# Weight sums of the FFN's down projection in half blocks on another engine, and the layer norm's channel sums as split matmuls

## The chip, the cores and the metric

The kernel runs on one core of a Trainium2 chip. The metric is the device time of one execution in microseconds (us). The core has five engines that run side by side, each with its own queue of instructions, worked off in order: TensorE (PE, matmuls), VectorE (DVE), ScalarE (ACT), GpSimd (POOL) and SyncE (SP, which here only starts DMA transfers). SBUF is the on-chip memory that the engines work from, PSUM the memory into which TensorE writes its products, and DRAM the large memory outside.

## What is computed

One residual block on x of 512 frames by 1024 channels, all in float32:

```
h   = rmsnorm(x); proj = h @ w_in                      # 1024 -> 8208 columns
a   = gated delta rule over 8 heads of 128, chunks of 64, then rmsnorm and silu(z)
c   = ga * sigmoid(gb); c = causal depthwise conv of 31 taps (c) + bias
c   = silu(layernorm over the 1024 channels (c))       # mean and variance of each frame
x   = x + (gate_a * (a @ w_o) + gate_b * (c @ w_pw2 + b)) @ w_out
h2  = rmsnorm(x)
f   = silu(h2 @ w_gate) * (h2 @ w_up)                  # 1024 -> 2 x 2816
out = rmsnorm(x + f @ w_down)                          # 2816 -> 1024
```

## The kernel before

**Products.** Activations lie with channels on the 128 partitions and the 512 frames along the free axis (128x512 tiles). A product in float32 accuracy is made of three faster ones: each operand is split into a rounded half (type fp32r) and the rest, `hi` and `lo`, and `split3` (L117) multiplies hi·hi, hi·lo and lo·hi. For weights this is done by `unit` (L101): SP loads 128x1024 into `raw`, ACT copies it rounded into `whi` (L113), DVE subtracts to get `wlo` (L114). The pool `wp` has three buffers of each, so the load of a unit waits until DVE is through with the `raw` of three units before, and the copy into `whi` waits until TensorE is through with the old one.

**Layer norm.** The convolution of 31 taps runs on DVE in the background of the first stage and ends in eight tiles `cv`; DVE adds them up into `sacc` (L704). Behind the first of eight column blocks of `a @ w_o`, `ln_mean` (L715) multiplies `sacc` by a matrix of ones, so that every partition holds the sum over the channels; it subtracts the mean and adds up the squares in `vacc`. Behind the fourth block `ln_norm` (L731) does the same with `vacc`, and scales. These two matmuls (L717, L733) take plain float32 operands and run as two instructions each. The tile name `acc4` is that of the short convolution's accumulators, two buffers in the pool `tp`.

**FFN.** Both FFN products use a recursive scheme that saves one of eight block products, for which sums and differences of weight blocks are needed. For gate and up, DMAs that add as they write make these sums in DRAM (`s1` to `s4`). For down, `w_down` comes in 11 row blocks k of four 128x512 sub-blocks each; `dsums_load` (L168) loads them, `dsums_add` (L171) makes four sums in place, and a DMA from POOL's queue stores them to `wsum[k]` in DRAM. That is done in 22 half blocks `halves` (k and one half of 512 columns) where there is room: 14 of them before the FFN, in buffers called `U` and `wsh`. The eight left (`rest`, k = 7 to 10) are done while gate and up run.

That stage is a loop over pairs f = 3 to 21 (L1180): `pair(f)` takes four units (loads from `wgu` and `s1` to `s4`; the last of the four has 128x512) and seven products of 12 matmuls with 256 columns; `dsums_to(f)` (L1069) does a part of `rest`; `some_operands(f)` makes the rounded halves `fh` and `fl` of finished hidden tiles `fm`, from f = 11 on with a difference `s` on DVE and two operations on POOL ahead. Before, `dsums_to` takes whole blocks of 128x4x512 in f = 8, 11, 14 and 17, in one buffer `wst`: the load on SP behind the last unit of the pair, the four sums and the store on POOL.

**Order.** The program is written once for all engines; each engine gets its instructions in about the order of the source, moved by priorities, and waits on semaphores for its inputs and for the buffers that it writes. `tc.issue_after(x)` keeps an instruction behind x on the same engine, and `behind()` behind the last marked ones of each engine.

Of the kernel before, what the change touches and what calls it, by code (L numbers as in the profile page):

```python
# [6 lines left out]
F32 = mybir.dt.float32  # L7
F32R = mybir.dt.float32r
I32 = mybir.dt.int32
AF = mybir.ActivationFunctionType  # L10
ALU = mybir.AluOpType
# [3 lines left out]
P = 128  # L15
T = 512
# [16 lines left out]
def block_kernel(ctx, tc, a):  # L33
    nc = tc.nc
    V, S, G, PE = nc.vector, nc.scalar, nc.gpsimd, nc.tensor
# [16 lines left out]
    ident, tri, suf, mid, ones, neg = (cst[:, i * P:(i + 1) * P] for i in range(6))  # L52
# [17 lines left out]
    one = small.tile([P, 1], F32, name="one")  # L70
# [14 lines left out]
    def marked(b, kind="drain"):  # L85
        mark[b.ins.engine, kind] = b.ins
        return b

    @contextmanager
    def behind(only=None):  # L90
        with ExitStack() as st:
            for i in list(mark.values()):
                if only is None or i.engine == only:
                    st.enter_context(tc.issue_after(i))
            yield
# [35 lines left out]
    psm = ctx.enter_context(tc.tile_pool(name="psm", bufs=3, space=PSUM))  # L131
# [4 lines left out]
    tp = keep.enter_context(tc.tile_pool(name="tp", bufs=2))  # L136
# [7 lines left out]
    cs = []  # L144
# [23 lines left out]
    def dsums_load(k, r, eng, cs=slice(0, T)):  # L168
        eng.dma_start(r, a["wdn"][k].rearrange("p (i c) -> p i c", i=4)[:, :, cs])

    def dsums_add(k, r, cs=slice(0, T)):  # L171
        b11, b12, b21, b22 = (r[:, i, :] for i in range(4))
        with tc.issue_after(last[0].ins):
            for o, x, y in ((b22, b12, b22), (b12, b11, b12), (b11, b22, b11), (b21, b11, b21)):
                G.tensor_tensor(out=o, in0=x, in1=y, op=ALU.add)  # L175
        nc.gpsimd.dma_start(wsum[k][:, :, cs], r)

    def half_load():
# [24 lines left out]
    def fill():  # L203

        units[0] += 1
        if units[0] % 3 != 2 or not gps_:
            feed_one()
        if taken and units[0] % 3 != 2 and not norming[0]:
            dsums_add(*taken.pop(0))
        if halves and gps_ and units[0] > 3 and not taken and not norming[0] and (units[0] % 2 == 0 if len(gps_) == 1 else units[0] % 3 == 0):  # L210
            half_load()
# [3 lines left out]
    with tc.tile_pool(name="st", bufs=2) as st:  # L215
# [78 lines left out]
        ps = psg.tile([P, 4, P], F32, name="g")  # L294
# [8 lines left out]
        raw, hi, lo = early[3]  # L303
# [41 lines left out]
        for k in range(2, 4):  # L345
# [6 lines left out]
                        in1=ss[:, 1].rearrange("p (n a) -> p n a", a=1).broadcast_to([P, NT, 16]), op=ALU.mult)  # L352
# [6 lines left out]
                        in1=rowp[:, 1:2, :].broadcast_to([P, NT, H]), op=ALU.add)  # L359
# [9 lines left out]
        with tc.issue_after(ln_.ins):  # L369
            for g_ in gated:  # L370
# [8 lines left out]
                        op=ALU.mult)  # L379
# [313 lines left out]
    sacc = tp.tile([P, T], F32, name="sacc", bufs=1)  # L693
# [14 lines left out]
    def gate(i):  # L708
# [3 lines left out]
        nc.sync.dma_start(sgd[i], sg)  # L712
        yield

    def ln_mean():  # L715
        ps = psm.tile([P, T], F32, name="mm")
        PE.matmul(ps, ones, sacc, start=True, stop=True)  # L717
        mu = tp.tile([P, T], F32, name="pa", bufs=1)
        S.activation(mu, ps, AF.Copy, scale=1.0 / D)
        vacc = tp.tile([P, T], F32, name="sacc", bufs=1)  # L720
        for i in range(KD):
            V.tensor_tensor(out=cv[i], in0=cv[i], in1=mu, op=ALU.subtract)
            if i == 0:
                S.activation(vacc, cv[i], AF.Square)
            else:
                sq2 = tp.tile([P, T], F32, name="acc4")
                S.activation(sq2, cv[i], AF.Square)
                V.tensor_tensor(out=vacc, in0=vacc, in1=sq2, op=ALU.add)
        return vacc

    def ln_norm(vacc):  # L731
        ps = psm.tile([P, T], F32, name="mm")
        PE.matmul(ps, ones, vacc, start=True, stop=True)  # L733
        rstd = tp.tile([P, T], F32, name="pa", bufs=1)
        S.activation(rstd, ps, AF.Sqrt, scale=1.0 / D, bias=epsc)
        V.reciprocal(out=rstd, in_=rstd)
        for i in range(KD):
            V.tensor_tensor(out=cv[i], in0=cv[i], in1=rstd, op=ALU.mult)
            S.activation(cv[i], cv[i], AF.Silu, scale=ln_w[:, i:i + 1], bias=ln_b[:, i:i + 1])
# [102 lines left out]
    def others():  # L842
        for i in range(2, KD):
            yield from glu(i)
        yield from gates(0, 16)
# [9 lines left out]
    rest = others()  # L855
# [30 lines left out]
    mp = ph2.enter_context(tc.tile_pool(name="mp", bufs=2))  # L886
    mp.tile([P, PAD], F32, name="pad", bufs=1)
    while taken:
        dsums_add(*taken.pop(0))
# [8 lines left out]
    def split(src):  # L898
        hi = mp.tile([P, T], F32R, name="yh", bufs=KD)
        lo = mp.tile([P, T], F32R, name="yl", bufs=KD)  # L900
        S.activation(hi, src, AF.Copy)
        V.tensor_tensor(out=lo, in0=src, in1=hi.bitcast(F32), op=ALU.subtract)
        return hi, lo

    mas = []
    oh, ol = zip(*[split(zall[:, k, :]) for k in range(KD)])
    for j in range(KD):
        if j == 1:
            vacc = ln_mean()
        if j == 4:  # L910
            ln_norm(vacc)
            norming[0] = False
        ps = psm.tile([P, T], F32, name="mm")
        col_tile(ps, a["wo"][j], oh, ol)
        ma = mp.tile([P, T], F32, name="ma", bufs=KD + 1)
        V.tensor_tensor(out=ma, in0=ps, in1=gate_of(j), op=ALU.mult)
        mas.append(ma)
# [7 lines left out]
    for j in range(KD):  # L925
        ps = psm.tile([P, T], F32, name="mm")
# [92 lines left out]
    while taken:  # L1019
        dsums_add(*taken.pop(0))  # L1020
    gps_.clear()
    rest = [(k, cs) for k, cs in halves]
# [5 lines left out]
    TH, KH = T // 2, KD // 2  # L1028
    t1, t2 = slice(0, TH), slice(TH, T)
    fp = ctx.enter_context(tc.tile_pool(name="fp", bufs=FF))  # L1030
    fs = ctx.enter_context(tc.tile_pool(name="fs", bufs=1))
# [10 lines left out]
    def tt(out, in0, in1, op, eng=V):  # L1042
        return eng.tensor_tensor(out=out, in0=in0, in1=in1, op=op)  # L1043
# [9 lines left out]
    def operands(f):  # L1053
# [12 lines left out]
        tt(b[:, t2], b[:, t1], b[:, t2], ALU.subtract, G)  # L1066
        tt(b[:, t1], b[:, t2], fm[:, t2], ALU.add, G)

    def dsums_to(f):  # L1069
        if f > 7 and f % 3 == 2 and rest:  # L1070
            k, cs = rest.pop(0)
            if rest and rest[0][0] == k:
                rest.pop(0)
                cs = slice(0, T)
            r = fs.tile([P, 4, T], F32, name="wst")[:, :, 0:cs.stop - cs.start]
            with tc.issue_after(loads[-1].ins):
                dsums_load(k, r, nc.sync, cs)
            dsums_add(k, r, cs)

# [36 lines left out]
    for f in range(F0):  # L1118
        start_feed[0] = f > 0
        dsums_to(f)  # L1120
        if f > 1:
            pg = psm.tile([P, T], F32, name="mm")
            col_tile(pg, a["wgu"][f], hhk, hlk)
        else:
            pg = first[2 * f][0]
            k_loop(*first[2 * f], slice(2 * P, T))
        sg = fq.tile([P, T], F32, name="cw", bufs=2)
        S.activation(sg, pg, AF.Silu)
        if f:
            next_todo()  # L1130
            pu = psm.tile([P, T], F32, name="mm")
            col_tile(pu, a["wgu"][FF + f], hhk, hlk)
        else:
            pu = first[1][0]
            k_loop(*first[1], slice(2 * P, T))
        tt(hidden(), pu, sg, ALU.mult)
        next_todo()
# [42 lines left out]
    for f in range(F0, FF):  # L1180
        pair(f)
        dsums_to(f)
        some_operands(f)
# [155 lines left out]
    for c, b in ((0, bank), (256, bank2)):  # L1339
        ps = b()[:, c:c + 256]  # L1340
        for k in range(K0, FK):
            part(k, 1, ps, c, 256, k == K0, k == FK - 1)
        cs = slice(T + c, T + c + 256)
# [65 lines left out]
```

## Time and profile before

| | before |
|---|---|
| time, median of 3 runs (lowest, highest) | 935.79 us (934.35, 938.48) |
| the profiled execution: its own time | 935.9 us |
| its span, first to last instruction | 934.1 us |
| mean granted TensorE clock | 0.998 |
| ACT busy, POOL busy | 566.6 us, 360.7 us |
| `wst` adds on POOL, 128x512 | 16, 1.36 us in the median, from 681.1 to 781.7 |
| stores `wsum<-wst`, 1 MB | 4, 5.8 us from issue to landing |

The profile is of one execution. A row of a timeline gives the start in us from the span's start, the duration of what stands in it, the engine, the line, the operation, the tiles as out<-in, the shapes, a count, and in brackets how long the engine had been idle and whose end ended that. The chain that ended last is followed back from the last instruction, at each step to what released it; its rows have the start, the length and the work.

### The profile page before, as it was taken

Reading aid. Unit: us, or ns where it says so; the run is one execution under the profiler, and the core shown is the slowest. Engines: PE = TensorE matmul, PEld = TensorE weight load, DVE = VectorE, ACT = ScalarE, POOL = GpSimd, SP = SyncE. Lnnn points to the kernel's source line nnn. Section 1 sums busy time; section 2 is a strip of 40 time slices with the busy share of each in tenths; the row PEclk is TensorE's granted clock in tenths of the full one; section 3 lists DMA queues with packets and bytes.
Section 4 is the critical chain, followed back from the end, with each engine's and each line's share of the span. In section 5 each row is a group of like instructions: output and inputs, shape, how many; then the busy total and the mean of one; then the engine's idle time right before and its main releaser. Section 6 shows DMA issues by size and latency. Waiting matters only on the chain.

```text
span 934.1 us, 15301 instructions
## 1 busy us (share of the span) xinstructions
PE 919.9 (98%) x5204; PEld 792.2 (85%) x5204; DVE 766.8 (82%) x1205; ACT 566.6 (61%) x1292; POOL 360.7 (39%) x572
## 2 busy tenths in 40 slices
PE   9999999999999999999999999999999999999997
PEld 6788788888888888888888888989999999988886
DVE  4999898898989989998587643876787888889896
ACT  7697977889778796642555323354444444556545
POOL 0145476363653438445155342211033234144042
PEclk9999999999999999999999999999999999999999
DMA  9335765674664556978999998689677767677654
GB/s 326 113 115 176 192 191 154 154 187 116 181 158 122 159 146 193 304 249 261 298 275 290 297 249 215 198 213 262 204 256 244 261 217 259 189 241 254 210 183 153
DMA packets 90286, 197.62 MB, mean 212 GB/s; under 512 B 11424, under 2 KB 20816, under 8 KB 89184
## 3 DMA queue, kind: packets, MB, share of 16 engines
q1 hardware_dynamic: 75168, 161.93, 50.9%
q0 software_dynamic: 13744, 32.05, 17.7%
q10 hardware_dynamic: 1296, 2.67, 0.7%
q8 instruction: 41, 0.67, 0.3%
q14 instruction: 37, 0.30, 0.1%
HBM read 176.40 MB, written 60.05 MB: 253 GB/s over the span
## 4 chain that ended last, share of the span: by engine, by line
PE 70%; ACT 11%; DVE 9%; DMA 3%; issue 2%; POOL 0%; SPq 0%; POOLq 0%; ACTq 0%; DVEq 0%
PE mm L123 43%; PE w L123 21%; DVE wlo L114 4%; ACT whi L113 2%; DMA raw<-s 2%; PE b L531 2%; DVE acc L425 1%; DMA raw<-in_wgu_dram 1%; DVE cw L1043 1%; PE g L438 1%; DVE cps L699 1%; PE st L644 1%; ACT s L549 1%; ACT Un L482 1%; ACT Vp L517 1%
## 5 line engine op out<-in xcount | busy, mean ns | idle before, releaser
L113 ACT ACTIVATE whi<-raw 128x1024 fp32r<-128x1024 f32 (+1 forms) x205 | 208.0, 1016 | 213.0 <-PE mm L123 114.6
L114 DVE TENSOR_TENSOR wlo<-raw,whi 128x1024 fp32r<-128x1024 f32 (+1 forms) x205 | 259.0, 1264 | 73.5 <-ACT whi L113 69.4
L123 PE MATMUL mm<-hh,whi 128*128 128x512 f32 (+1 forms) x612 | 235.6, 386 | 0.8 <-DVE acc L425 0.4
L123 PE MATMUL mm<-hh,wlo 128*128 128x512 f32 (+1 forms) x612 | 230.3, 377 | 0.0
L123 PE MATMUL mm<-hl,whi 128*128 128x512 f32 (+1 forms) x612 | 229.4, 375 | 0.0
L699 DVE SCALAR_TENSOR_TENSOR cps<-c,c31w,cps 128x512 f32<-128x512 f32 x224 | 167.8, 749 | 3.6
L123 PEld LDWEIGHTS mm<-hh,wlo 128*128 128x128 f32 x612 | 115.5, 189 | 19.0
L123 PEld LDWEIGHTS mm<-hh,whi 128*128 128x128 f32 x612 | 115.7, 189 | 17.9 <-issue 1.0
L123 PEld LDWEIGHTS mm<-hl,whi 128*128 128x128 f32 x612 | 115.8, 189 | 16.1
L123 PE MATMUL w<-hh,wlo 128*128 128x256 f32 x244 | 69.6, 285 | 1.5 <-DVE wlo L114 1.5
L199 POOL DMA_DIRECT2D s<-s x38 | 33.5, 882 | 93.6 <-DMA s<-in_wgu_dram 86.4
L199 POOL DMA_DIRECT2D s<-in_wgu_dram x38 | 32.9, 876 | 93.7 <-DMA s<-in_wgu_dram 81.9
L123 PE MATMUL w<-hh,whi 128*128 128x256 f32 x244 | 69.1, 284 | 0.0
L123 PE MATMUL w<-hl,whi 128*128 128x256 f32 x244 | 69.0, 283 | 0.0
L1043 POOL TENSOR_TENSOR fm<-fm 128x256 f32<-128x256 f32 x33 | 34.6, 1051 | 72.6 <-DVE s L1043 51.1
L425 DVE SCALAR_TENSOR_TENSOR acc<-mm,c4w,acc 128x511 f32<-128x511 f32 (+2 forms) x72 | 53.0, 741 | 2.5 <-ACT acc L422 2.4
L507 POOL TENSOR_TENSOR ytm<-U,y 128x60 f32<-128x60 f32 (+14 forms) x120 | 34.3, 286 | 47.0 <-DMA U<-sc 36.1
L175 POOL TENSOR_TENSOR wst<-wst 128x512 f32<-128x512 f32 x16 | 24.6, 1537 | 70.5 <-DMA wst<-in_wdn_dram 38.8
L123 PE MATMUL mm<-yh,whi 128*128 128x512 f32 x128 | 50.6, 396 | 0.0
L123 PE MATMUL mm<-yh,wlo 128*128 128x512 f32 x128 | 49.8, 389 | 0.0
L123 PE MATMUL mm<-yl,whi 128*128 128x512 f32 x128 | 49.8, 389 | 0.0
L123 PEld LDWEIGHTS w<-hh,wlo 128*128 128x128 f32 x244 | 46.8, 192 | 2.3 <-DVE wlo L114 2.1
(343 smaller groups left out, 2152.3 us busy)
## 6 DMA issues: line engine op xcount, KB each, us to landing
raw<-in_win_dram SPq DMA_DIRECT2D x61, 512.0 KB, 4.3
s<-in_wgu_dram SPq DMA_DIRECT2D x76, 256.0 KB, 5.5
raw<-s SPq DMA_DIRECT2D x76, 256.0 KB, 4.1
raw<-in_wgu_dram SPq DMA_DIRECT2D x25, 512.0 KB, 4.4
raw<-wsum SPq DMA_DIRECT2D x44, 256.0 KB, 3.7
s<-in_wgu_dram POOLq DMA_DIRECT2D x38, 256.0 KB, 6.0
s<-s POOLq DMA_DIRECT2D x38, 256.0 KB, 5.6
raw<-in_wdn_dram SPq DMA_DIRECT2D x33, 256.0 KB, 3.3
```

What stands on the lines that cost most here:

```text
L113: marked(S.activation(hi, raw, AF.Copy), "unit")
L114: marked(V.tensor_tensor(out=lo, in0=raw, in1=hi.bitcast(F32), op=ALU.subtract), "unit")
L123: marked(PE.matmul(ps, l, r, start=first and i == 0, stop=last and i == 2))
L175: G.tensor_tensor(out=o, in0=x, in1=y, op=ALU.add)
L199: fed.append(nc.gpsimd.dma_start(*begun.pop(0), accum_op=ALU.add, max_dma_last_dim=2048))
L425: marked(V.scalar_tensor_tensor(out=acc[:, s:], in0=ps[:, :T - s], scalar=c4w[:, j, k:k + 1], in1=acc[:, s:], op0=ALU.mult, op1=ALU.add))
L438: PE.transpose(ps[:, n, :], src[:, n, :], ident)
L482: S.activation(Un[:, n, :], ps[:, n, :], AF.Copy, scale=nb2[:, n:n + 1])
L507: G.tensor_tensor(out=tm[:, :, 0:w], in0=U[:, k, :, k + 1:], in1=y[:, :, k:k + 1].broadcast_to([P, NT, w]), op=ALU.mult)
L531: PE.matmul(ps[:, q, 0:w], stationary[:, q, :], moving[:, q, :], start=True, stop=True)
L699: V.scalar_tensor_tensor(out=acc if k < 30 else cv[i], in0=c[:, k:k + T], scalar=c31w[:, i, k:k + 1], in1=acc if k > 1 else cv[i], op0=ALU ...
L1043: return eng.tensor_tensor(out=out, in0=in0, in1=in1, op=op)
```

## The change

There are two parts. The eight half blocks that are left for the gate and up stage stay half blocks: from f = 4 to f = 11 each pair loads one into one of two buffers `wst` of 128x4x256, and the pair after it makes the four sums on DVE instead of POOL; the store is still issued by POOL. And the layer norm's two sums over channels take their operand split into a rounded half and the rest, in two `acc4` buffers each, times a rounded copy of the ones, which makes two matmuls of the fast kind for each sum; the split of `sacc` is written ahead of those of `zall`.

```diff
-    def dsums_add(k, r, cs=slice(0, T)):
+    def dsums_add(k, r, cs=slice(0, T), eng=G):
         b11, b12, b21, b22 = (r[:, i, :] for i in range(4))
         with tc.issue_after(last[0].ins):
             for o, x, y in ((b22, b12, b22), (b12, b11, b12), (b11, b22, b11), (b21, b11, b21)):
-                G.tensor_tensor(out=o, in0=x, in1=y, op=ALU.add)
+                eng.tensor_tensor(out=o, in0=x, in1=y, op=ALU.add)
         nc.gpsimd.dma_start(wsum[k][:, :, cs], r)
...
+    def halves_of(src):
+
+        hi, lo = (tp.tile([P, T], F32, name="acc4").bitcast(F32R) for _ in range(2))
+        S.activation(hi, src, AF.Copy)
+        V.tensor_tensor(out=lo, in0=src, in1=hi.bitcast(F32), op=ALU.subtract)
+        return hi, lo
+
+    def over_channels(hi, lo):
+
+        ps = psm.tile([P, T], F32, name="mm")
+        marked(PE.matmul(ps, one_, hi, start=True, stop=False))
+        marked(PE.matmul(ps, one_, lo, start=False, stop=True))
+        return ps
+
     def ln_mean():
-        ps = psm.tile([P, T], F32, name="mm")
-        PE.matmul(ps, ones, sacc, start=True, stop=True)
+        ps = over_channels(*sums_)
...
     def ln_norm(vacc):
-        ps = psm.tile([P, T], F32, name="mm")
-        PE.matmul(ps, ones, vacc, start=True, stop=True)
+        ps = over_channels(*halves_of(vacc))
...
     mas = []
+    one_ = mp.tile([P, P], F32R, name="one", bufs=1)
+    S.activation(one_, ones, AF.Copy)
+    sums_ = halves_of(sacc)
     oh, ol = zip(*[split(zall[:, k, :]) for k in range(KD)])
...
+    landed = []
+
     def dsums_to(f):
-        if f > 7 and f % 3 == 2 and rest:
+        if landed:
+            with behind():
+                dsums_add(*landed.pop(0), eng=V)
+        if f > 3 and rest:
             k, cs = rest.pop(0)
-            if rest and rest[0][0] == k:
-                rest.pop(0)
-                cs = slice(0, T)
-            r = fs.tile([P, 4, T], F32, name="wst")[:, :, 0:cs.stop - cs.start]
+            r = fs.tile([P, 4, TH], F32, name="wst", bufs=2)
             with tc.issue_after(loads[-1].ins):
                 dsums_load(k, r, nc.sync, cs)
-            dsums_add(k, r, cs)
+            landed.append((k, r, cs))
```

The new lines shift the line numbers behind them: L1040, L1043 and L1178 of before are L1055, L1058 and L1195 in the changed kernel.

On DVE, in pair f = 8 from the third product's sum to the first low part of the next pair, the program of before has (`wlo` is a unit's low part, `fl` the low part of a hidden tile):

```order
L1043 TENSOR_TENSOR cw<-cu,w 128x256
L1043 TENSOR_TENSOR fm<-w,cv_7460 128x512
L1043 TENSOR_TENSOR cw<-cw,w 128x512
L114 TENSOR_TENSOR wlo<-raw,whi 128x1024
L1178 SCALAR_TENSOR_TENSOR fm<-fm,cw 128x512
L114 TENSOR_TENSOR wlo<-raw,whi 128x512
L1040 TENSOR_TENSOR fl<-fm,fh 128x256
L114 TENSOR_TENSOR wlo<-raw,whi 128x1024
```

and the changed one, at the same place:

```order
L1058 TENSOR_TENSOR cw<-cu,w 128x256
L1058 TENSOR_TENSOR fm<-w,cv_7488 128x512
L1058 TENSOR_TENSOR cw<-cw,w 128x512
L114 TENSOR_TENSOR wlo<-raw,whi 128x1024
L1195 SCALAR_TENSOR_TENSOR fm<-fm,cw 128x512
L114 TENSOR_TENSOR wlo<-raw,whi 128x512
L1055 TENSOR_TENSOR fl<-fm,fh 128x256
L175 TENSOR_TENSOR wst<-wst 128x256 x4
L114 TENSOR_TENSOR wlo<-raw,whi 128x1024
```

Four adds of half width have come in between `fl` and the first low part of pair 9.

On SP, behind the last unit of pair f = 8 (`raw<-s_125`), the program of before loads a whole block once and then two pairs' units with no other load:

```order
L108 DMA raw<-s_125 128x512
L169 DMA wst<-in_wdn_dram 128x2048
L108 DMA raw<-in_wgu_dram 128x1024
L108 DMA raw<-in_wgu_dram 128x512
L108 DMA raw<-s_126 128x512
L108 DMA raw<-s_128 128x512
L108 DMA raw<-s_127 128x512
L108 DMA raw<-s_125 128x512
L108 DMA raw<-in_wgu_dram 128x1024
```

and the changed one a half block behind each pair:

```order
L108 DMA raw<-s_125 128x512
L169 DMA wst<-in_wdn_dram 128x4x256
L108 DMA raw<-in_wgu_dram 128x1024
L108 DMA raw<-in_wgu_dram 128x512
L108 DMA raw<-s_126 128x512
L108 DMA raw<-s_128 128x512
L108 DMA raw<-s_127 128x512
L108 DMA raw<-s_125 128x512
L169 DMA wst<-in_wdn_dram 128x4x256
L108 DMA raw<-in_wgu_dram 128x1024
```

The load of f = 6 and each one after it waits on SP for the store of the half block two pairs before, which leaves its buffer; the next pair's units stand behind it.

On POOL, in the pairs up to f = 12, the adds stood before between the stores and, from f = 11 on, the operations on the hidden tiles `fm`:

```order
L175 TENSOR_TENSOR wst<-wst 128x512 x4
L176 DMA wsum<-wst 128x2048
L175 TENSOR_TENSOR wst<-wst 128x512 x4
L176 DMA wsum<-wst 128x2048
L1043 TENSOR_TENSOR fm<-fm 128x256 x4
L175 TENSOR_TENSOR wst<-wst 128x512 x3
L1043 TENSOR_TENSOR fm<-fm 128x256
L175 TENSOR_TENSOR wst<-wst 128x512
```

Now only the stores are left there:

```order
L199 DMA s_126<-s_125 128x512
L199 DMA s_128<-s_126 128x512
L176 DMA wsum<-wst 512x1x256 x7
L1058 TENSOR_TENSOR fm<-fm 128x256 x2
L176 DMA wsum<-wst 512x1x256
```

The sixteen adds are gone from POOL, and eight stores stand where there were four.

## The prediction

> **What bounds the kernel now.** I read the page's busy shares first, then the chain that ended last in order of time, then the timelines of VectorE (DVE), GpSimd (POOL) and SyncE (SP) in the stage that the change touches.
>
> ```profile
> span 934.1 us, 15301 instructions
> PE 919.9 (98%) x5204; PEld 792.2 (85%) x5204; DVE 766.8 (82%) x1205; ACT 566.6 (61%) x1292; POOL 360.7 (39%) x572
> ```
>
> TensorE is the bound: nothing can be won but by giving it less work or by closing the few gaps in it. The chain shows where they are. A pair of the FFN (one f) takes four loads and seven products, 84 matmuls; two pairs repeat as one pattern.
>
> ```profile
> 462.31 0.86 PE mm L717 x2
> 463.17 16.36 PE mm L123 x72
> ...
> 627.20 11.51 PE w L123 x96
> ...
> 687.67 11.52 PE w L123 x96
> ...
> 755.29 5.10 DMA raw<-s
> ...
> 811.78 40.82 PE w L123 x219
> ```
>
> The pattern starts at 627.20 (pair f=3) and again at 687.67 (f=9): 60.47 us for six pairs, 10.08 for one (and 96 products in 11.52 are 0.12 each, 84 of them 10.08). Pair f=21, the last, starts at 811.78. Eighteen pairs at 10.08 are 181.4, which would end at 808.6, so **3.1 us** of waiting lie in between, all behind 687. A table by stretches of 10 us (busy time of PE, PEld, DVE, ACT, POOL; clock; DMA share; GB/s) agrees: PE is full in the 640s and 660s and not in the 740s and 780s.
>
> ```profile
> 640.00:650.00 10.00, 10.00 (x86) 10.00 (x85) 6.23 (x10) 3.95 (x7) 1.39 (x2) 1.00 0.95 281
> ...
> 660.00:670.00 10.00, 10.00 (x86) 10.00 (x85) 7.67 (x13) 5.25 (x9) 0.00 (x0) 1.00 0.53 188
> ...
> 740.00:750.00 10.00, 9.59 (x80) 9.38 (x79) 9.41 (x12) 5.35 (x8) 6.03 (x5) 1.00 0.77 278
> ...
> 780.00:790.00 10.00, 9.25 (x77) 9.04 (x76) 9.08 (x13) 3.88 (x7) 6.68 (x7) 1.00 0.57 205
> ```
>
> What delays DVE is seen in its timeline, first at f=7, then f=8, then f=14, and in POOL's:
>
> ```profile
> 671.54 0.69 DVE L114 TENSOR_TENSOR wlo<-raw,whi 128x512 fp32r<-128x512 f32 x1
> 672.14 0.42 DVE L1040 TENSOR_TENSOR fl<-fm,fh 128x256 fp32r<-128x256 f32 x1
> 674.33 1.23 DVE L114 TENSOR_TENSOR wlo<-raw,whi 128x1024 fp32r<-128x1024 f32 x1 [1.77 <-ACT whi L113]
> ...
> 681.62 1.78 DVE L114 TENSOR_TENSOR wlo<-raw,whi 128x512 fp32r<-128x512 f32 x1
> 683.32 1.52 DVE L1040 TENSOR_TENSOR fl<-fm,fh 128x256 fp32r<-128x256 f32 x1
> 684.76 2.31 DVE L114 TENSOR_TENSOR wlo<-raw,whi 128x1024 fp32r<-128x1024 f32 x1
> ```
>
> ```profile
> 744.08 1.51 DVE L1043 TENSOR_TENSOR s<-fm 128x256 f32<-128x256 f32 x1
> ...
> 747.02 2.25 DVE L114 TENSOR_TENSOR wlo<-raw,whi 128x1024 fp32r<-128x1024 f32 x1
> ```
>
> ```profile
> 681.14 7.09 POOL L175 TENSOR_TENSOR wst<-wst 128x512 f32<-128x512 f32 x4 [30.89 <-DVE wlo L114]
> ...
> 743.81 4.38 POOL L175 TENSOR_TENSOR wst<-wst 128x512 f32<-128x512 f32 x3 [6.59 <-DMA wst<-in_wdn_dram]
> ...
> 775.84 4.18 POOL L175 TENSOR_TENSOR wst<-wst 128x512 f32<-128x512 f32 x3 [7.13 <-DMA wst<-in_wdn_dram]
> ```
>
> While POOL adds, each DVE operation with both inputs in SBUF takes about 1.1 us longer: 0.69 becomes 1.78, 0.42 becomes 1.52, 1.23 becomes 2.31. Three or four in a row make DVE some 3.3 us late; the low parts `wlo` come late, the `raw` buffers come free late, the next load starts late, and PE waits. The PE gaps of the 740s and 780s stand right behind the POOL blocks of 744 and 776.
>
> **The change, part by part.** *The sums over channels.* A float32 matmul against ones costs 0.86; a rounded-half matmul costs 16.36 / 72 = 0.227, two of them 0.45. Two sums save 2 x (0.86 - 0.45) = **0.8 us**, and PE has work on both sides, so it is won in full. The price is one ACT copy and one DVE subtraction per sum, of 128x512.
>
> ```profile
> 440.61 0.69 DVE L704 TENSOR_TENSOR sacc<-sacc,cv 128x512 f32<-128x512 f32 x1
> ...
> 446.40 1.23 DVE L114 TENSOR_TENSOR wlo<-raw,whi 128x1024 fp32r<-128x1024 f32 x1 [3.97 <-ACT whi L113]
> ...
> 475.73 1.21 DVE L114 TENSOR_TENSOR wlo<-raw,whi 128x1024 fp32r<-128x1024 f32 x1
> 479.57 0.69 DVE L916 TENSOR_TENSOR ma<-mm,gsl 128x512 f32<-128x512 f32 x1 [2.64 <-PE mm L123]
> ```
>
> `sacc` is ready at 441.3, twenty us ahead of its matmul, and its split (0.69 like the addition) falls into an idle 3.97. `vacc` is ready before 475.7, its matmul is due at 463.17 + 16.36 = 479.5, and DVE idles 2.64 in between: 0.69 fits. I cost both at nothing; without that cover it would be at most 0.7 each.
>
> *The POOL adds go.* Sixteen adds leave POOL, and with them the 1.1 us on their neighbours. What is late next? Late pairs without a POOL block show it:
>
> ```profile
> 800.08 1.35 DVE L114 TENSOR_TENSOR wlo<-raw,whi 128x1024 fp32r<-128x1024 f32 x1 [0.33 <-ACT whi L113]
> ...
> 809.48 1.35 DVE L114 TENSOR_TENSOR wlo<-raw,whi 128x1024 fp32r<-128x1024 f32 x1 [0.33 <-ACT whi L113]
> ```
>
> From one pair's first low part to the next are 9.4 us, less than PE's 10.08, so undisturbed pairs gain on PE even with the heavier operands of f>10. I count **all 3.1 us** as won; the other end is none of it.
>
> *The adds come to DVE.* Eight blocks of four adds of 128x256 at 0.42 (`fl` at 672.14 has the same size and two SBUF inputs) are 1.7 us per pair, in f=5 to f=12. They stand behind `fl`, ahead of the next pair's first `wlo`: there DVE idles 1.77 at f=7. Where the gap is smaller, the first `wlo` may be late by the slack it has: it ends at 675.56 for pair f=8, which PE starts at 627.20 + 5 x 10.08 = 677.60, 2.0 us later. Their data landed ten us before. Cost nothing; uncovered at most 1.7 once. POOL issues the stores and has nothing else queued behind them until the `fm` operations of f=11.
>
> *More loads and stores, earlier.* This is the part that adds a wait. SP's queue at f=8, and the landing times:
>
> ```profile
> 671.43 4.48 SPq L108 DMA_DIRECT2D raw<-s  x4
> 676.07 0.33 SPq L169 DMA_DIRECT2D wst<-in_wdn_dram  x1
> 678.46 2.99 SPq L108 DMA_DIRECT2D raw<-in_wgu_dram  x2
> ```
>
> ```profile
> raw<-s SPq DMA_DIRECT2D x76, 256.0 KB, 4.1
> raw<-in_wgu_dram SPq DMA_DIRECT2D x25, 512.0 KB, 4.4
> ...
> wsum<-U POOLq DMA_DIRECT2D x8, 512.0 KB, 6.0
> ...
> wsum<-wsh POOLq DMA_DIRECT2D x6, 512.0 KB, 4.7
> ```
>
> Two buffers of 512 KB take turns. What is loaded at f=8 (676.07) is added a pair later, behind `fl` (672.14 + 0.42 + 20.16 = 692.7) until 694.4; its store, of the form of the `wsum<-U` and `wsum<-wsh` rows, lands 4.7 to 6.0 later, at 699.1 to 700.4. The load of f=10 wants that buffer at 676.07 + 20.16 = 696.2, so SP stands 2.9 to 4.2 us. Behind it stands the next pair's first load, due at 698.6: with 0.33 to issue the block it goes out 0.8 to 2.1 late, which the 2.0 us just about cover.
>
> Does the lateness grow? ScalarE's high parts `whi` are
>
> ```profile
> 666.04 1.06 ACT L113 ACTIVATE whi<-raw 128x1024 fp32r<-128x1024 f32 x1 [1.56 <-PE mm L123]
> ...
> 670.51 0.62 ACT L113 ACTIVATE whi<-raw 128x512 fp32r<-128x512 f32 x1
> ```
>
> From a landed store to the next store of that buffer: issue 0.33, first load 4.4, high part 1.06 and low part 1.23, last load 4.1, its high and low part 0.62 and 0.69, `fl` 0.42, adds 1.68, hand-overs some 0.3, store 4.7 to 6.0: 19.5 to 20.8, against two pairs of 20.16. So the **ring is about closed**: at 6.0 it slips 0.6 a turn, with two turns in six blocked loads.
>
> The Trainium skill, "DMA: Bandwidth & Descriptors", section "Anatomy of one DMA — SWDGE (gpsimd) path", fits a GpSimd-issued transfer by 2.0 us and bytes / 436e3, 3.2 us for 512 KB as an estimate; by that the ring takes 18.0 and no first load is late. The rows here, 4.7 and 6.0, are longer and decide. The same fit speaks against the change: eight such stores are 25.6 us and four of 1 MB 17.6.
>
> The transfers also come in a busier stretch, where the second low part of f=5 stands:
>
> ```profile
> 648.11 1.23 DVE L114 TENSOR_TENSOR wlo<-raw,whi 128x1024 fp32r<-128x1024 f32 x1 [1.27 <-ACT whi L113]
> ```
>
> In the 640s the DMA share is 0.95; 512 KB more at 281 GB/s are 1.9 us. That low part ends at 649.34 and PE wants it two of seven products into the pair, at 627.20 + 2 x 10.08 + 2.88 = 650.24: 0.9 us of slack, so up to 1.0 may be lost once. For all new waits together I take 0.8 us, near the row of 4.7 and the half-empty DMAs of the 660s. The ends are 0 (nothing in the new waits can make PE faster) and 5.3: with 6.0 for the store and both raw loads 0.5 later, the first load is 2.1 + 1.0 late, slips twice by 0.6 + 1.0, has 2.0 of slack, and f=5 adds 1.0.
>
> **Sum**, against the profiled execution's own 935.9 us (span 934.1 and 1.8 around it; the median of the three is 935.8): 935.9 - 0.8 - 3.1 + 0.8 = **932.8**.
>
> **The rivals.**
>
> 1. *The ring gives it back.* SP waits for stores, first loads come late, and PE waits at f=7 to f=13 instead of f=11 to f=18. For it: the ring at 20.8 against 20.16, and 1 MB more DMA per pair. Against it: a share of 0.53 in the 660s, and slack of 2.0. Half of its 5.3 and more: 935 to 937, say 935.5.
> 2. *Slower: the ring opens.* One place, SP's wait for the store ahead of the first load. The slowest of these stores took 7.8:
>
> ```profile
> wsum<-U POOLq DMA_DIRECT2D x1, 512.0 KB, 7.8
> ```
>
> The first load is then 3.9 late and the ring 22.6, slipping 2.4 a turn: 3.9 + 4.8 - 2.0 + 1.0 = 7.7 lost, 932.0 + 7.7 = 939.7. It decides once a store lands later than about 6.5. Against it: that row stands in another stage, with more traffic.
> 3. *The gaps stay.* The chain's longest pieces in them are DMAs (5.10 of `raw<-s`); were these the cause and not POOL, only the 0.8 of the sums is won: 935.1. Against it: 4.1 is that load's median, and f=19 to 21 run without a gap.
>
> The change not doing what it says would look like the third.
>
> **How the numbers follow.** Chances: forecast (931.5 to 934) 0.57, first rival 0.20, second 0.09, third 0.14. The sum cannot go below 932.0, but the three times of before spread from 934.35 to 938.48, so a measured 931 is possible. The range, 930.8 to 937.0, takes in the forecast, the third and most of the first, and leaves out the second. Half a per cent, 4.7 us, is about what a measurement of this kernel can tell from no change: faster by more 0.10, within 0.84, slower by more 0.06.
>
> **What would show it.** Right: no POOL `wst` rows; no DVE `wlo` of 1024 above 1.5 between 680 and 800; the sums at 0.45 each in the chain; pair f=21 starting 181.5 to 182.3 after f=3. SP's wait ahead of `wst` loads near 3 to 4 us from f=6 on. Wrong: PE waiting for `wlo` at f=7 to f=13 with `raw<-in_wgu_dram` issued over 2 us late (first two rivals), or gaps left at f=13 to 18 with short DVE rows (third).

## The result and the profile after

The changed kernel takes 942.08 us in the median of 11 runs (938.13 to 946.04), the kernel before 936.76 in 11 runs beside it: ratio 1.0051, interval 1.0032 to 1.0071. The change makes the kernel slower by half a per cent, against a forecast of 932.8 in a range of 930.8 to 937.0. The profiled execution has the median's time. One run of `parts_two` below, of 2340 us, is left out of its numbers. Head of the page of the changed kernel:

```profile
span 939.8 us, 15334 instructions
PE 920.2 (98%) x5204; PEld 792.1 (84%) x5204; DVE 770.7 (82%) x1239; ACT 568.8 (61%) x1295; POOL 333.9 (36%) x560
```

PE's busy time is the same within 0.3 us, and POOL, without the adds, has 27 us less; so the time has gone into waiting. The chain that ended last, of the changed kernel (start, length, work):

```profile
464.17 0.23 PE mm L725
464.40 0.23 PE mm L726
...
628.71 8.53 PE w L123 x71
...
642.76 8.90 DMA raw<-s
651.77 1.07 ACT whi L113
652.86 1.24 DVE wlo L114
654.14 7.11 PE w L123 x57
...
667.10 6.64 DMA raw<-s
673.85 1.07 ACT whi L113
674.93 1.24 DVE wlo L114
676.22 7.11 PE w L123 x57
...
690.74 0.35 DVE wst L175
...
699.14 6.45 DMA raw<-s
...
716.83 11.53 PE w L123 x94
...
737.00 11.52 PE w L123 x96
...
817.64 12.47 PE w L123 x94
```

Pair f = 3 starts at 628.71, f = 21 at 817.64: 188.93 us for 18 pairs, where before took 811.78 - 627.20 = 184.58 and 18 x 10.08 are 181.4. So 7.5 us are waited. Eight pairs from 737.00 to 817.64 take 80.64, which is 8 x 10.08: **nothing is lost behind f = 11**, where the kernel before lost its 3.1. On PE's timeline all 7.5 lie at f = 5 to f = 11, where the blocks are now: 2.4 at f = 5 and 5.1 behind it. The chain goes the same way each time: a unit's load (mostly `raw<-s`, half of a pair's second unit) lands late, then come its high part and its low part. Even the new adds stand in it, at 690.74. PE itself stands at the start of a pair for 6.0 of the 7.5 us, waiting for the high or low part of the pair's first unit (f = 5, 7, 8, 10 and 11), and for the low part of a second unit for 1.6 (f = 5 and 7). PE's timeline of the changed kernel at f = 7 and f = 8; the first and the last row are a first unit's, the middle one a second unit's:

```profile
672.72 0.38 PE L123 MATMUL w<-hh,wlo 128*128 128x256 f32 x1 [0.75 <-DVE wlo L114]
...
676.22 0.38 PE L123 MATMUL w<-th,wlo 128*128 128x256 f32 x1 [0.37 <-DVE wlo L114]
...
684.60 0.39 PE L123 MATMUL w<-hh,wlo 128*128 128x256 f32 x1 [0.76 <-DVE wlo L114]
```

The wait that the prediction feared is there too. From SP's waits of the changed kernel (what waits, for what: us in total, times, longest) and its DMA issues (count, KB, median us to landing):

```profile
SPq L169 <- DMA wsum<-wst: 15.4, 6, 3.7
```

```profile
raw<-s SPq DMA_DIRECT2D x76, 256.0 KB, 3.8
...
wsum<-wst POOLq DMA_DIRECT2D x8, 512.0 KB, 4.7
```

### The profile page after: what moved, and what is told of

It reads as the page before. It is cut to its first block, busy times and chain, and to the rows that moved or that the text cites. A ratio compares the mean times of both kernels' runs of the same rounds, so it can differ in the third digit from the quotient of the medians.

```text
span 939.8 us, 15334 instructions
## 1 busy us (share of the span) xinstructions
PE 920.2 (98%) x5204; PEld 792.1 (84%) x5204; DVE 770.7 (82%) x1239; ACT 568.8 (61%) x1295; POOL 333.9 (36%) x560
## 4 chain that ended last, share of the span: by engine, by line
PE 75%; ACT 8%; DVE 6%; DMA 4%; issue 2%; POOL 0%; SPq 0%; POOLq 0%; ACTq 0%; DVEq 0%
PE mm L123 46%; PE w L123 22%; DVE wlo L114 2%; DMA raw<-s 2%; PE b L531 2%; ACT whi L113 2%; PE g L438 1%; DMA s<-in_wgu_dram 1%; PE st L644 1%; DMA raw<-in_wgu_dram 1%; PE g L479 1%; DVE acc L425 1%; ACT s L549 1%; PE st L635 1%; DVE cw L1058 0%
## 5 line engine op out<-in xcount | busy, mean ns | idle before, releaser
L114 DVE TENSOR_TENSOR wlo<-raw,whi 128x1024 fp32r<-128x1024 f32 (+1 forms) x205 | 251.1, 1226 | 73.5 <-ACT whi L113 68.7
L1058 POOL TENSOR_TENSOR fm<-fm 128x256 f32<-128x256 f32 x33 | 30.1, 913 | 103.1 <-DVE s L1058 80.6
L507 POOL TENSOR_TENSOR ytm<-U,y 128x60 f32<-128x60 f32 (+14 forms) x120 | 38.2, 318 | 46.4 <-DMA U<-sc 38.2
L123 PEld LDWEIGHTS w<-hh,whi 128*128 128x128 f32 x244 | 46.7, 192 | 1.2 <-ACT whi L113 1.1
```

The costliest lines, as they stand in the source:

```text
L114: marked(V.tensor_tensor(out=lo, in0=raw, in1=hi.bitcast(F32), op=ALU.subtract), "unit")
L123: marked(PE.matmul(ps, l, r, start=first and i == 0, stop=last and i == 2))
L507: G.tensor_tensor(out=tm[:, :, 0:w], in0=U[:, k, :, k + 1:], in1=y[:, :, k:k + 1].broadcast_to([P, NT, w]), op=ALU.mult)
```

## The experiments

Below, "stage" is the time from the first product of f = 3 to the first one of the down projection, on PE's timeline of one profiled execution: 194.7 before, 199.0 after. It scatters from one execution to the next (`sums_only`, whose code for the stage is that of before, has 196.3), and so do the stages ahead of it, so times are compared by the ratio to runs of before on the same chip.

| run | SP waits for stores, us | stage, us | median, us | ratio to before, interval |
|---|---|---|---|---|
| sums_only | none | 196.3 | 937.13 | 0.9995 (0.9979 to 1.0012) |
| down_only | 14.9 | 197.7 | 940.83 | 1.0042 (1.0025 to 1.0060) |
| loads_on_pool | none on SP | 195.5 | 937.97 | 1.0002 (0.9978 to 1.0025) |
| every_second | none | 191.6 | 933.80 | 0.9957 (0.9939 to 0.9975) |
| second_from_4 | none | 193.2 | 936.26 | 0.9986 (0.9968 to 1.0004) |
| two_pairs_later | 13.9 | 196.6 | 938.09 | 0.9999 (0.9981 to 1.0017) |
| every_second_pool | none | 192.6 | 935.70 | 0.9976 (0.9957 to 0.9995) |
| halves_on_pool | none | 194.9 | 938.34 | 1.0002 (0.9981 to 1.0022) |
| early_adds | 2.1 | 199.2 | 941.61 | 1.0037 (1.0014 to 1.0060) |
| early_adds_later | 2.3 | 195.6 | 938.01 | 1.0022 (1.0005 to 1.0040) |
| load_behind_w46 | none | 199.7 | 940.17 | 1.0010 (0.9992 to 1.0028) |
| off_load | none | 191.5 | 934.63 | 0.9971 (0.9958 to 0.9984) |
| off_adds | none | 193.4 | 935.33 | 0.9977 (0.9959 to 0.9995) |
| off_adds_store | none | 193.8 | 936.96 | 0.9990 (0.9973 to 1.0007) |
| off_all | 17.7 | 198.3 | 941.08 | 1.0040 (1.0018 to 1.0061) |
| parts_two | 20.6 | 191.5 | 934.51 | 0.9962 (0.9938 to 0.9987) |
| parts_three | none | 191.7 | 933.85 | 0.9955 (0.9933 to 0.9976) |

### The two halves of the change

`sums_only` is the kernel before with the layer norm's part alone, `down_only` with the half blocks alone.

> The kernel before with the layer norm's sums alone as split matmuls; the down sums as before. Whatever made the changed kernel slow in the gate and up stage, this part should only save: about 0.8 us against before (ratio 0.999), the stretch from the first block of a @ w_o to the transposes shorter by 0.8 us, and pair f=21 starting 184.6 us after f=3 as before. If the extra 1.9 us that the changed kernel's profile shows ahead of 450 us belongs to this part and not to the run, the ratio is above 1.001.

> The kernel before with the eight half blocks on VectorE alone; the sums over channels as before. If all of the loss lies in the gate and up stage, as the profile after has it (188.9 us from f=3 to f=21 against 184.6 before and 181.4 without a wait), this is about 5 to 6 us slower than before (ratio 1.006), 0.8 us more than the whole change.

The loss belongs to the half blocks: `down_only` has it and `sums_only` does not. That `down_only` would be 0.8 us slower than the whole change does not show: its ratio is below the whole change's 1.0051, with intervals that overlap. The sums' 0.8 is too small for these times; the traces are read below.

### The place on the queue, and the spacing

```diff
# loads_on_pool, against the changed kernel
-                dsums_load(k, r, nc.sync, cs)
+                dsums_load(k, r, nc.gpsimd, cs)
# every_second
-        if f > 3 and rest:
+        if f > 4 and f % 2 and rest:
# second_from_4
-        if f > 3 and rest:
+        if f > 3 and f % 2 == 0 and rest:
# two_pairs_later
-        if f > 3 and rest:
+        if f > 5 and rest:
```

> The changed kernel with the loads of the half blocks issued from GpSimd's queue, so that SyncE no longer stands still for the stores; the transfers, the buffers and the adds are the same. Theory 1 (SyncE's wait holds up the next pair's first load): the stalls at f=7 to f=11, some 5 us, go, those at f=5 (2.4 us) stay; about 937 us. Theory 2 (the extra transfers slow the units' loads, whoever issues them): all stays, about 942 us. Theory 3 (the adds on VectorE make the low parts late): about 942 us.

> The changed kernel with a half block in every second pair, f=5, 7, ..., 19, added in the pair after. No load then waits for a store, none lies in f=4 beside the last of the feeding DMAs, and the transfers per pair are halved; the adds on VectorE are the same in number, four of them now beside the heavier operands of f>10. Theories 1 and 2: nearly no stall is left, f=3 to f=21 in 181.5 to 183 us, time 933 to 936 us, under before. Theory 3: pairs above 10 need 9.4 + 1.7 us against TensorE's 10.1 every second time, stalls of 0.5 us or more per pair there, 937 to 942 us.

> The changed kernel with blocks loaded in every second pair as in the run every_second, but from f = 4 on (f = 4, 6, ... 18) instead of f = 5. Two causes, each its own: the block load at f = 4 stands among the last feeding DMAs, so the gap of some 2.4 us at f = 5 stays and nothing follows it: about 936.2 (933.8 of every_second plus 2.4). Rival, the queue alone: the block load at f = 4 is harmless when no store is waited for behind it: no gap in the stage, about 933.8. Third, the early gap starts the rest: gap at f = 5 and again at f = 7 to f = 9, about 938.

> The changed kernel with a block in each pair still, but from f = 6 to f = 13 instead of f = 4 to f = 11, behind the feeding DMAs. If the waits of SP for the stores are a cause of their own, SP stands some 3 us per pair from f = 8 on, the first loads come late and PE loses 3 to 5 us at f = 9 to f = 13: about 938 to 939.7. If the late start at f = 5 causes all of it, the two buffers come free in time and there is no gap: about 934.

With a block in every second pair, nothing is lost. The chain of `every_second` in the stage is PE alone:

```profile
462.62 0.23 PE mm L725
...
626.64 11.51 PE w L123 x96
...
808.14 22.01 PE w L123 x136
```

18 pairs in 181.50 us, the forecast's 181.4. `second_from_4` keeps the spacing and begins at f = 4: it loses 1.7 us of stage, all at f = 5, behind a `raw<-s` of 8.34 us in its chain. `two_pairs_later` begins behind the feeding DMAs (those that make `s1` to `s4`), loses nothing at f = 5, and 5.0 us of stage, nearly all at f = 10 to f = 14. So there are two losses, about 2 at f = 5 and about 5 behind it, and either comes without the other.

`loads_on_pool` takes the wait away from SP and is faster than the changed kernel, 1.0002 against 1.0051 with intervals that do not meet, but PE still waits 3.9 us. The edit did one thing more than was meant: the first two blocks leave POOL's queue at 601 and 603, ahead of the stage, where the changed kernel loads them at 638 and 651. Against what was expected, the loss at f = 5 is gone (0.2), and 3.7 of the 5.1 behind it stay. Its chain shows the loop that sets the pace there:

```profile
675.76 5.04 DMA raw<-s
680.90 1.07 ACT whi L113
681.99 1.23 DVE wlo L114
684.06 0.68 DVE cw L1058
684.74 1.15 DVE wlo L114
686.29 4.54 DMA raw<-s
690.93 1.07 ACT whi L113
692.03 1.23 DVE wlo L114
694.78 1.15 DVE wlo L114
696.32 4.87 DMA raw<-s
...
706.69 5.33 DMA raw<-s
```

The load of a pair's second unit leads to its high and low part; behind that low part and three sums stands the third unit's low part on DVE; it frees the `raw` buffer (three units before, with three buffers) that the second unit of the next pair is loaded into. One turn is one pair. From 675.76 to 686.29 are 10.53 with a load of 5.04, then 10.03 with 4.54, then 10.37 with 4.87: **the load and 5.49**. PE's pair is 10.08, so that load has 4.6 us before the loop becomes slower than PE. In the median `raw<-s` takes 3.8 in the changed kernel, so the slack of a whole pair is 0.8.

### The engine of the adds

```diff
# halves_on_pool against the changed kernel, every_second_pool against every_second
-                dsums_add(*landed.pop(0), eng=V)
+                dsums_add(*landed.pop(0))
```

> The changed kernel, a half block in each pair from f = 4 on, with the adds on POOL. POOL is slower at an add (0.68 or more for 128x256, half of 1.36, against 0.42) and lengthens DVE's subtractions, so the way from load to stored block is at least 1.1 us longer and SP stands longer at each pair: 943 to 946. Rival: the adds on POOL need not stand behind DVE's fl, they start as soon as the load has landed and the store goes out sooner: SP's wait shrinks and the time is 937 to 940.

> The run every_second with the four adds of each half block on POOL instead of DVE. If only the even spacing of half blocks counted, the time stays at 933.8. If POOL's adds delay DVE as in the kernel before (each subtraction beside them about 1.1 us longer), half blocks of four short adds delay one or two subtractions per block: wlo rows of 2.3 us again, gaps of 0.2 to 0.5 at some of eight blocks, about 935 to 936.5.

`halves_on_pool` went by the rival: POOL adds as soon as a block has landed, SP never waits for a store, and behind f = 8 no gap is left, with the same loads and stores in each pair. Of its 3.4 us of waiting, 2.3 lie at f = 5. `every_second_pool` shows what POOL's adds cost DVE: the last unit's low part takes 1.22 in DVE's timeline, where it takes 0.69 alone, beside these adds in POOL's:

```profile
774.28 1.22 DVE L114 TENSOR_TENSOR wlo<-raw,whi 128x512 fp32r<-128x512 f32 x1
```

```profile
772.33 4.66 POOL L175 TENSOR_TENSOR wst<-wst 128x256 f32<-128x256 f32 x4 [5.39 <-DMA wst<-in_wdn_dram]
```

It loses 1.0 us of stage against `every_second`. By the medians it is 1.9 us behind `every_second`, with intervals that overlap.

### Without SP's wait

```diff
# early_adds: the adds written at the start of the next pair
 def pair(f):
     w = unit(a["wgu"][f])
     next_todo()
+    if landed:
+        with behind():
+            dsums_add(*landed.pop(0), eng=V)
# early_adds_later: the same with f > 5
# load_behind_w46: block_load is the second half of dsums_to, with f > 4
     w46 = unit((a["wgu"][FF + f][:, T:], s("s2")))
+    block_load(f)
...
     w5 = unit((s("s1"),))
+    if landed:
+        with behind():
+            dsums_add(*landed.pop(0), eng=V)
```

> The changed kernel, a half block in each pair from f = 4 to f = 11 still, its four adds still on DVE, but written at the start of the next pair, which puts them on DVE between the sums cu, cv2 and cw of the pair whose last load the block's load stands behind, and no longer behind fl. From load to adds it is then some 8 us shorter. If SP's wait for the stores is what the changed kernel lost behind f = 5, that wait goes to nothing and only the gaps at f = 5 stay: 935.5 to 936.5, as second_from_4. If the number of transfers is the cause, or DVE's extra 1.7 us per pair, it stays at 939 to 942; adds between cu and cw could also delay cw and fm and so TensorE's banks.

> As early_adds, with the blocks in f = 6 to f = 13, behind the feeding DMAs. With both causes away there is no gap in the stage and the time is that of every_second, 933.8, with a load, adds and a store in each pair. If transfers or DVE's work in each pair cost on their own, 936 to 938, near two_pairs_later (938.1).

> The changed kernel with one thing moved: on SP each block's load stands behind the loads of the next pair's first two units instead of ahead of them (in f = 5 to f = 12 of the source); the adds stay behind fl, the stores stay with them. If the loss behind f = 5 comes from SP holding back the next pair's first load, so that it, the block and the second unit's load leave together and the second unit lands 6.5 instead of 4 to 5 us later, then that second load now lands in 5.1 or less, the gaps behind f = 5 go, and the gap at f = 5 too, as the first block no longer stands ahead of that pair's loads: 934 to 935.5. If one more load and store in each pair (the DMAs' share of 0.8) or the 1.7 us of adds on DVE cost on their own, wherever they stand, gaps remain in most pairs: 938 to 941. The second pair of matmuls' weights w37 now stands behind the wait for the store: should that wait stay, gaps appear at the sixth product of a pair instead of the third.

My theory here was that SP's wait for the stores is the loss. As the whole of it, it fell: `early_adds` has 2.1 us of that wait and loses as much as the changed kernel, and `early_adds_later` is no faster than `two_pairs_later` by the ratios. As a part of it, it stands: `load_behind_w46`, like `loads_on_pool` and `halves_on_pool`, has no such wait and is some 4 us faster than the changed kernel by the ratios, with intervals that do not meet; but each of the three changed something else too, and none gets near `every_second`. The places of PE's waits behind f = 5 point the same way. With SP's wait they are at a pair's first unit, whose load stands right behind the block on SP: 4.5 of 5.1 us in the changed kernel, all of them in `two_pairs_later` and `off_all`. Without it most are at later units in `early_adds` (all but 1.2 of 5.2) and `loads_on_pool` (all but 1.3 of 3.7); the 1.2 of `halves_on_pool` are at first units. The chain of `early_adds` runs through the loop of `loads_on_pool`, with one add in it:

```profile
658.26 4.82 DMA raw<-s
...
667.02 0.34 DVE wst L175
667.36 1.15 DVE wlo L114
...
668.89 6.08 DMA raw<-s
...
680.79 4.97 DMA raw<-s
...
691.59 5.04 DMA raw<-s
```

Turns of 10.63, 11.90 and 10.80, which is the load and 5.82: 5.49 and the add's 0.34. The load of 6.08 left 1.2 us behind a store (POOL issues it at 667.66). In `load_behind_w46` the second unit's data land in time and the third unit's do not: its low part comes 3.1 to 6.0 us behind the second's in f = 6 to f = 12, against 2.66 where it is not held up. This kernel takes the block away from one unit's load and puts it beside another's. (Its profile is of an execution of 944.6 us, well above its median, in which the clock also fell to 0.96 for 40 us, so its stage is not compared further.)

### One thing at a time

To see which part of a block costs, one part was added to the free pairs of `every_second`: `off_load` loads each next block a pair early into its own buffer and then again; `off_adds` takes four maxima of a sub-block with itself, which change nothing; `off_adds_store` stores the block again behind them; `off_all` does all three.

```diff
+        if again and f % 2:
+            k, r, cs = again.pop(0)
+            with behind(), tc.issue_after(last[0].ins):
+                for i in range(4):
+                    V.tensor_tensor(out=r[:, i, :], in0=r[:, i, :], in1=r[:, i, :], op=ALU.max)
+            nc.gpsimd.dma_start(wsum[k][:, :, cs], r)
...
+        elif f > 4 and f % 2 == 0 and rest:
+            ready.append(fs.tile([P, 4, TH], F32, name="wst", bufs=2))
+            with tc.issue_after(loads[-1].ins):
+                dsums_load(rest[0][0], ready[0], nc.sync, rest[0][1])
```

> The run every_second (933.8 us, no gap in the stage) with one more load of 512 KB in each pair that had none, f = 6 to f = 18, at the same place on SP; what it loads is overwritten by the next block and not used. If a load in each pair holds up the units' loads, the second unit's data come more than 5.1 us behind the last low part and TensorE waits in the even pairs too: 936 to 940. If the load is harmless and the loss comes of the adds or of the store, 933.8 to 934.5.

> The run every_second with four more DVE operations of the size of the adds (the maximum of each sub-block with itself, which changes nothing) in each pair that had none, f = 7 to f = 21, behind fl as the adds. If 1.7 us on DVE in each pair leave no time to recover, 936 to 940. If the adds are hidden as the prediction had it, 933.8.

> The run off_adds with the block stored a second time behind the added operations, so that each pair has four operations on DVE and a store of 512 KB, but only each second pair a load. If the store is what lengthens the units' loads, 3 to 6 us above off_adds; if not, the same as off_adds.

> The loads of off_load and the operations and stores of off_adds_store together: each pair from f = 7 to f = 18 then has what each pair of the changed kernel has, but no load ever waits for a store. If the loss comes of having all three in each pair and not of that wait, 940 to 945, with raw<-s loads of over 5 us; if the wait is needed for it, 934 to 936.

By the ratios these are 1.3, 1.9, 3.1 and 7.8 us above `every_second`; the intervals of the first two overlap its own widely and that of `off_adds_store` at its edge. In the profiles PE waits 0, 1.8, 2.3 and 6.7 us in the stage, and 1.0 of the 1.8 of `off_adds` lies at f = 5, ahead of the first added operation. So a load alone has no price that shows, the adds alone cost at most 0.8 in the trace, and the store 0.5 to 1.2 on top of `off_adds`, less than the 3 to 6 that I had expected of a store that is the cause. All three together cost 6.7 to 7.8, more than the sum. But `off_all` does wait for stores on SP, against what was expected of it (its buffers come free a pair later than those of `off_load`), so its 6.7 to 7.8 hold that wait too:

```profile
SPq L169 <- DMA wsum<-wst: 17.7, 6, 4.3
```

### Smaller blocks, and the wait by itself

```diff
+    parts = [(k, slice(c, min(c + 192, T))) for k in sorted({k for k, _ in rest}) for c in (0, 192, 384)]
...
-        if f > 3 and rest:
-            k, cs = rest.pop(0)
-            r = fs.tile([P, 4, TH], F32, name="wst", bufs=2)
+        if f > 5 and parts:
+            k, cs = parts.pop(0)
+            r = fs.tile([P, 4, 192], F32, name="wst", bufs=2)[:, :, 0:cs.stop - cs.start]   # parts_three: bufs=3
```

> The eight half blocks as twelve parts of 192 or 128 columns, one in each pair from f = 6 to f = 17 (behind the feeding DMAs), load, adds and store placed as in the changed kernel, two buffers. A part's store lands about as late as a half block's, so SP waits for it as in two_pairs_later, some 1 to 3 us per pair: 936.5 to 939, with gaps in the middle of the stage.

> parts_two with a third buffer and nothing else changed: SP no longer waits for a store. If that wait is what costs, by holding back the next pair's first load, 934 to 935, two us or more under parts_two. If it is only a sign, and the load, adds and store in each pair cost wherever SP stands, within half a us of parts_two.

The same work in twelve parts of 384 or 256 KB, one in each pair, loses next to nothing in either profile (0 and 0.2 us), against the 936.5 to 939 that I had expected, though SP waits for stores longer in `parts_two` than in any other run. SP's waits and DMA issues of `parts_two`:

```profile
SPq L169 <- DMA wsum<-wst: 20.6, 10, 3.4
```

```profile
raw<-s SPq DMA_DIRECT2D x53, 256.0 KB, 3.8
...
wsum<-wst POOLq DMA_DIRECT2D x8, 384.0 KB, 3.6
...
wsum<-wst POOLq DMA_DIRECT2D x4, 256.0 KB, 2.5
```

A third buffer takes all of that wait away and wins 0.7 us by the medians, with intervals that overlap. Against `two_pairs_later`, which begins in the same pair and has the same two buffers with blocks of 512 KB, `parts_two` wins 5.0 us of stage and 3.5 us by the ratios, with intervals that just overlap. SP's wait is about the same, 2.1 us each time against 2.3. So a wait of 2.1 us per pair is covered there; 512 KB each way and 1.7 us of adds in each pair, with that wait, are not. `every_second` and `parts_three` are the fastest kernels here, 0.4% faster than before; both keep the new sums over channels and DVE's adds.

## Why the prediction was wrong, step by step

- **The sums over channels: right in price, not always won in full.** A sum takes two pieces of 0.23, where it took 0.86. From the first sum to f = 3 `every_second` takes 626.64 - 462.62 = 164.02 us, before 627.20 - 462.31 = 164.89: 0.87 won for 0.8 forecast. But the low half of `vacc` was counted as covered, and it is ready in time by little. In five of the 17 profiles with the new sums, that of `sums_only` among them, PE waits 0.44 us for it, which is half of the gain. PE's timeline of `sums_only`:

```profile
479.22 0.50 PE L726 MATMUL mm<-acc,one 128*128 128x512 f32 x1 [0.44 <-DVE acc L719]
```

  In the changed kernel it does not wait there, but once, later, for a load `s`, and the stretch takes 164.54.
- **POOL's adds go, all 3.1 us won: right in size, the cause only in part shown.** `every_second`, which has half blocks as far as f = 20, runs the whole stage at PE's pace. But its blocks are also half as large as before and twice as many. With the same half blocks added on POOL, `every_second_pool` loses 1.0 us, so about 1.0 is the engine's share; the rest went with the smaller blocks, and the third rival's DMAs are not ruled out as part of it. The 3.1 itself is that of one profile: the same code in `sums_only` lost 4.7.
- **The adds on DVE cost nothing: not borne out.** The idle 1.77 ahead of a pair's first low part is there, but it is not free time for each pair. The prediction has the data landed ten us before. The load for that part goes out at 668.38, when the low part of three units before has freed its buffer, and takes 3.5 us to land; the copy to `whi`, which PE releases, starts at 673.24, only 1.3 us later. SP's and ACT's timelines of before:

```profile
668.38 2.99 SPq L108 DMA_DIRECT2D raw<-in_wgu_dram  x2
```

```profile
673.24 1.06 ACT L113 ACTIVATE whi<-raw 128x1024 fp32r<-128x1024 f32 x1 [1.17 <-PE w L123]
```

  DVE's own low parts let the loads go, so what is put ahead of a low part pushes a later load. In the changed kernel the adds stand in the chain at 690.74, and in `early_adds` one of them lengthens each turn of the loop by 0.33. Their price alone is small, at most 0.8 us in the trace of `off_adds`.
- **New waits, 0.8 us, at most 5.3: this term failed; with the adds it measures 7.5.** SP's wait itself was sized about right: 2.9 to 4.2 forecast, 2.6 in the mean and 3.7 at most. The ring was 21.1 and 22.2 in two turns rather than 19.5 to 20.8 (SP's `wst` loads of one buffer stand at 676.34 and 697.41, and 686.03 and 708.18), and f = 5 lost 2.4 where I had 1.0. What failed is the slack of 2.0 us that I set against it. It takes all that stands ahead of the first unit's load as on time and the load as 4.4 us. In the changed kernel that load goes out 2.4 and 2.5 us after its buffer came free for f = 7 and f = 10, 0.9 and 0.8 for f = 8 and f = 11, and takes 4.2 to 5.5. And the buffer itself comes free late: it is freed by the low part of the second unit of the pair before, whose load has only 4.6 us in its loop for a transfer of 3.8, so 0.8 us of slack, and goes out with what was held back. So the lateness of one pair runs into the next, and PE waits 6.0 us at first units and 1.6 at second ones. The low part that frees the buffer for f = 7, in DVE's timeline of the changed kernel, and SP's timeline behind it:

```profile
662.43 1.23 DVE L114 TENSOR_TENSOR wlo<-raw,whi 128x1024 fp32r<-128x1024 f32 x1 [0.30 <-ACT whi L113]
```

```profile
665.33 0.59 SPq L169 DMA_DIRECT2D wst<-in_wdn_dram  x1
666.08 0.97 SPq L108 DMA_DIRECT2D raw<-in_wgu_dram  x2
667.10 5.91 SPq L108 DMA_DIRECT2D raw<-s  x4
```

  The buffer is free at 663.66 and the first unit's load leaves at 666.08. Block, first unit and second unit, 1.5 MB, leave within 2 us, and the second unit's `raw<-s` takes 6.64, which is 2.0 more than it has.
- **Rival 2 was the nearest** in place and size, 939.7 at a chance of 0.09, but that is luck in part, because its point of decision was wrong: it asked for stores landing later than about 6.5 us, and in the changed kernel they land in 4.7 in the median and 6.5 at most. SP's wait is also not needed for a loss, as `early_adds` shows, and not enough for one, as `parts_two` shows.

Shown: the loop and its 4.6 us; that in the changed kernel PE waits mostly for first units, whose loads SP holds back; that the loss is in the half blocks; that it goes with free pairs or smaller blocks; that load, adds and store together cost far more than any of them alone. Open: how the 7.5 divide between SP's bunching and the shared DMAs, because the parts don't add up and `off_all` has both; and whether three whole buffers of 512 KB would do, which was not tried.

## What to carry to other kernels

When work is put into "idle" places of a loop, ask first what the idle engine waits for: if that wait ends a loop through its own earlier instruction, the idle time is the loop's slack, and the least slack of all loops counts, not that at the place of the insert. Work out such a loop as fixed part plus load, per turn, before spending it. And spreading side work evenly over all turns is not always gentle: work in every second turn, or in smaller pieces, lost nothing here, where whole pieces in each turn did.

## What the runs showed of the hardware

At one size a transfer's time depended much on its company: 256 KB of `raw<-s` took 3.8 us in the median, 6.64 beside 1.25 MB that left with it, and 8.90 in the 640s, where the window of the changed kernel shows a DMA share of 1.05:

```profile
640.00:650.00 10.00, 9.36 (x76) 8.95 (x75) 4.92 (x7) 3.95 (x6) 1.63 (x2) 1.00 1.05 305
```

GpSimd-issued stores of 256, 384 and 512 KB landed in 2.5, 3.6 and 4.7 us in the median, the first two in `parts_two` and the last in the changed kernel; those of 512 KB went from 3.8 in `off_load` to 6.2 in `load_behind_w46`. The Trainium skill, "DMA: Bandwidth & Descriptors", section "Anatomy of one DMA — SWDGE (gpsimd) path", has a fixed 2.0 us and bytes / 436e3 on top, by which they would take 2.6, 2.9 and 3.2 us as an estimate; the trace agrees for the smallest alone.
